# A new fixed order of all steps, and a new buffer table, for the two mixing stages of a two-layer hybrid decoder

## The chip, the core and the metric

The kernel runs on one core of one Trainium2 chip. Five engines work from queues of their own and in the order in which the program puts instructions into them: TensorE (PE, with its weight loads shown apart as PEld), VectorE (DVE), ScalarE (ACT), GpSimd (POOL) and SyncE (SP), which issues most transfers. An instruction waits at the head of its queue until the semaphores of what it needs are set; everything behind it in that queue waits too. The metric is the device time of one execution in microseconds, lower is better. Three runs of the kernel before took 1265.35, 1265.58 and 1265.79 us.

## The reference

Two layers over 512 tokens of width 1024, in float32. Each layer has a mixing stage and an MLP; the mixing stage runs three kinds of heads side by side on one input projection.

```python
for l in range(DEPTH):                                   # DEPTH = 2
    h = rms_norm(x, norm_mix_g[l])
    proj = h @ w_in[l]                                   # 1024 -> 3328 columns
    p_att, p_conv, p_rwkv = jnp.split(proj, ...)
    o_att = diff_attention(q, k, v, lam, ...)            # 6 heads of 64, two softmaxes each, causal
    o_conv = short_conv(b_gate, c_gate, u, conv_w[l])    # 256 channels, 3 taps
    o_rwkv = rwkv7_time_mix(p_rwkv, ...)                 # 6 heads of 64, a recurrence over 512 steps
    mixed = jnp.concatenate([o_att, o_conv, o_rwkv], axis=-1)
    x = x + mixed @ w_out[l]
    h = rms_norm(x, norm_mlp_g[l])
    x = x + jnp.square(jax.nn.relu(h @ w_mlp_up[l])) @ w_mlp_down[l]
return rms_norm(x, final_norm_g)
```

The recurrence of the third kind of head is, for each head and step,

```python
sa = einsum('bhvk,bhk->bhv', state, -kk_t)
state = state * w_t + sa (x) (kk_t * a_t) + v_t (x) k_t
y_t = einsum('bhvk,bhk->bhv', state, r_t)
```

## The kernel before

All activations lie transposed: 128 channels on the partitions, 512 tokens along the free axis, eight tiles `x0` to `x7` for the width of 1024. A product keeps float32's precision with three matmuls on rounded operands: weights and activations are split into a first part (`hi`, rounded by a cast on ACT) and a second part (`lo`, what is left, a subtraction on DVE or POOL), and PE adds hi*hi, hi*lo and lo*hi in PSUM. Weights come in groups of 128 output columns. Half a group (four blocks of 128 x 128, 256 KB) is loaded into a `raw` tile, cast to `whi` and subtracted to `wlo`; each of the three tiles has three buffers, so that at most three half groups are on their way.

A layer has two parts. The MLP is written out in plain loops. The mixing stage is written as generators, each of which yields after every instruction or small group of instructions (a *step*). The function `drive` takes a string, `ORDER[l]`, in which a letter stands for a generator and a number behind it for so many of its steps: `R2 m g3` is two steps of `R`, one of `m`, three of `g`. It calls the generators in that order, and so sets the order in every engine's queue. Between engines the string fixes nothing; the semaphores do. The letters:

- `d` the loads of raw weights and constants (SP), `w` the casts to `whi` (ACT), `x` and `y` the subtractions to `wlo` on DVE and on POOL (the string `LO` says which half group goes to which)
- `m` the products, one matmul a step: 888 in each stage, which are the input projection (`pj`, 624), the output projection in two halves of 96 (`po`), and the first three groups of the MLP (`up`, 72)
- `e`, `q`, `n` the scaling and the RMS norm of the input; `k` constants
- `g`, `h` the decay rates and the gate of the recurrence
- `A`, `B`, `C` three pairs of attention heads; `U`, `V` the two convolution tiles
- `R`, `S`, `T` three pairs of recurrent heads, and `r`, `s`, `t` the triangular inverse that each of them needs
- `o`, `i`, `p`, `N` the residual sums, the scaling and the norm of the MLP's input

An attention pair handles two heads of four blocks of 128 queries. For each block PE makes two score tiles (`sc`); DVE adds the causal mask and finds the maximum (line 1298), ACT takes the exponentials with their sums (L1305), DVE makes the factor of the second softmax (`sm`, L1307 and L1309, one column wide) and the difference `pp` (L1311); PE transposes it (`ptt`), ACT copies it out, and after four blocks PE multiplies with the values (`po` of the attention, with 64 columns).

A recurrent pair works in chunks of 64 tokens. Its matmuls are on 64 x 64 parts of PE's array: gram matrices (`pg`), then `pbv`, `pzw`, `pap`, `pbs`, `pyy`; between them stand transposes (`pk`, `pb`, `pa`, `pv`, `phy`) and the seven state updates (`pst`). The inverse uses 64 x 64 and 32 x 32 parts (`px`, `py`, `pz`, `pzz`) and, on POOL, thirty small operations. A pair ends with a gate product (`pgt`), the output `yc` (L1101 and L1108) and its two parts `mhi` and `mlo` (L851 and L852), which the output projection reads. The order of the output projection's blocks is `K_ORD`: its second half starts with the outputs of `S`, `V`, `C` and `T`, in this order.

Beside the order stands a table, `SLOTS[l]`: for each tag with several buffers the sequence of buffer numbers in which tiles take them, such as `wp/wlo 012012...` or `ps/rp` for the four PSUM banks that the small work shares. The products have PSUM banks of their own (`ps/mm`, two), and so has attention (`ps/at`, two).

Of the kernel before, what the change touches and what calls it, by code (L numbers as in the profile page):

```python
# [22 lines left out]
S = 512  # L23
# [3 lines left out]
C = 64  # L27
# [28 lines left out]
         "g d6 e d2 w e q m w m w x2 d m w m d x m q m d e m q d m q e d m e d m q2 m d e m e d m q d w m2 d e m w m d m x m d m w m x d m2 x d m q m "  # L56
         "d m e m q d m2 d e2 m2 q d m e m e m2 q m2 e2 m2 q m e m3 q m3 q m2 k5 m k q m3 k m k n k m n m n m2 n m n m n w m n m n x w d m n x m2 w m "
         "d m2 g y m5 k g m d g m k2 m2 k m k g m3 g m3 g m2 w m g m g m x m3 g3 d g m3 g3 m2 w g2 A m3 x A m3 d A m2 A m2 A m g m3 w g2 h y m2 g m R "
         "m3 g d g R2 m2 g m R m w m2 g2 m g2 x m g2 R d m g m A m R m R m h m A m R m w m2 A2 m R m y m A m R A2 m d R m R m R A m R2 m A m w m A m2 "
         "x A m3 d m2 R m2 R m R m w m2 R m y m5 R2 m d m3 w A R m A m x A6 m A2 m R d A m2 R A m A2 m2 A m2 R m w m2 R m2 y R A d A m A R m A R m A2 "  # L60
         "R m r A2 m A m A m R2 w r A m R r x A d R6 A R h R r3 A R2 m h R h m A m R A2 m A2 m R m A m r A m r m R2 m A m2 w m A m r m A R m r R A y "
         "m3 A m r A2 d R2 A r A m2 r m A r A m2 r B m w r m2 r R2 A y B A m2 R m r d m R A m r A R m r R r A B2 R2 r m B A2 h w r2 m r A m r m A x m2 "
         "A m r d m A r m2 r A3 m r A m A r A m2 r w m r S m A m r m x S m S m r A m d A m r m A r m S A m A2 m w A2 m A m A m x m A m2 d m A m r A m "
         "A m2 A h m2 w S m2 A2 x m S h A m S A d m2 r m2 r m2 r m w m r2 m3 A m2 y m2 A r A m d S m r m r A m h w m r S A y B m r S B r d A m2 r3 A m "
         "S A2 B2 m r S B A2 r B m r2 m r B m r A2 B m r S B S2 m r2 m w r m B R S x B S2 m d S R m2 A R S m3 S A m R A S A2 R2 m A2 R5 A m R m A R m "
         "w R m R m A R y m R A m R m A m R d A m A R m A m A R A m A m R A m w A R A m A m R y R d S m R S m R m2 R m2 R m S m R m2 S w S A x A d B S "
         "m S B A s S m S2 B R m s m3 A m s S m2 A m3 w S2 A R x S m S B m R m A R s3 m R m R S d S R A R m B R m S R m B A m S m B S2 R s B R m s S m "
         "B s w B2 s T s x m T2 m s B m d B m s B m T m B m2 s B m S m3 s w m B s m B S m s m y B m B2 m B2 m B m B s d m S2 m B m2 w m B T m2 s m S B "
         "S m s B m T s m T m x B m s B2 d m T B m2 s B w m s m B T m s m y m B T B s m d T m B s T m T m s m B m s B m s w m C m s B s m S C S m s T "
         "B C2 T B m B s B m C s m2 s B2 m s m x m B m2 R d m R w m2 B m y R s m R2 d B m S T S T B m S T s m B S s m T m s m w m s2 m B2 C S y R C S "  # L70
         "B R s C2 B d m s T m s C m T m C m s B C R S m C B s T m C S m s B3 m s2 m s m B m w C B m s C B y m s m s3 m B m s d B m B s B m s2 m B s m "
         "B2 S w B2 S m2 B2 m2 U m B m2 S m2 B m x m S B d B2 S m B S B S m w B2 m2 B m B m S m B m S m S2 m B S m B m S2 B m2 w m S B S2 x B2 m y S d "
         "B2 S m B m B m d m S B U2 m S m S m U B m S m S2 w B2 T m S B T S m S B2 S T S m T m T B S B2 m x B m T B d m T m2 B t T m2 T2 B m t m w m C "
         "m t m y m T m C T2 C d B m S T B m S B m S T B m t3 S B m T S T B S B S B m S T B m S B m w S B m S B m T S B m2 T2 t y B T m C B m2 t C m T "
         "m C m2 t w C m S m C T m2 t V C2 t C S C T d C m C S2 C m t C m S t m2 t m C t m C m t w m x C m C2 m t d C2 m t C m C t m2 x C m2 t m d C m "
         "C m t C w m t m U C U t m x m C2 m t C2 d m t m C2 m t m U m C m2 t w m U m2 C t m2 C t m C m U m2 C m C2 t x m C w m C t d m t m C t m C m "
         "t m x m C m t m V d m V t m C t m V m w m4 C m y C m4 t C d m C2 m C m t w m2 C m t m t m C m t2 m C m B m T m2 C3 B w T m2 C t T C x m C T2 "
         "C d t m C m t T2 U C x t T C d m T U C T m t C2 m t C2 T C2 m t C m3 t C m w C m C m t2 y V C T t m t2 m t C2 m T d C2 S t C m C S m C m3 t "
         "m C t2 m C m w o m2 V y m C m2 t T d V C T m T C2 m C2 m T C2 V C V C m T m T m w T m2 o V m y m T m2 T m T2 m d C m T m C m2 w T2 C o m C2 "
         "T2 x T V d m C m T m C m T C m T m C m T C3 m T m2 C T C w m C T2 o C x m C d T C m C T m C m C T m2 C m T m2 C T m C2 m2 w m T m C y m o C "  # L80
         "m3 C m T d m T m T C m3 T w m T o m3 T x m3 T d m T m T m T m T m w T m T m2 o y m T m T2 d m T m4 T m2 w m T m2 o y m6 d m3 w m o m2 y m p "
         "m3 i m2 d m i m2 w m o m3 x p m3 d i p m5 w m i m2 o m3 x m p m2 d m p m2 w m o m2 y m p m4 p m d m3 w m o m3 x p m3 d p m5 w m o m3 x p m3 "
         "d p m5 w m o m2 y m p m4 p m d m i m3 w o m3 i2 m2 p m i m i m p m3 w m i2 N x m i2 m d m i2 m2 i m3 N m x m2 w m3 y m5 N m N m N m N m w N "
         "m N y m N m34 ",
         "d3 w e x q d e w q y d w m4 x m3 d m e g m d m q m d e m w m2 q m2 y m n m d n m n m2 n m n m n m n w m n y m n m3 d g m3 g m g m3 w g m3 x "
         "m3 d m3 g m3 g m2 w g m2 g m x m3 g3 d g m3 g3 m w m g2 x m3 d m4 g m3 g h g w m g R g3 m R2 m4 g2 m g2 R m g2 h m g m h m2 x m h w m2 d m h "
         "x m3 h d m3 h m3 w m R m2 h y m6 R h d R m3 w m R m2 R x m3 R d m R m R m R m R5 m R m2 w A m R m R m3 A m x m3 R d m2 w m3 R m3 R m5 R m w "
         "m2 R m2 R A2 x A x m d R m d m R m R m r m R2 m r m w m2 R r m2 R2 m x R m2 R m d m R2 r3 m R m2 R A R2 w R m A m R m3 A2 m R m2 r A m x m A "
         "m R m w A m2 A m2 A r m x m d m2 r A m r m A2 m r A r w d m r m A2 r R m2 A r m x m R A R m2 A r m r m A R2 A m r m d R2 r w r A r A R m A r "
         "m A R m x m R2 A r d r A m r R A m R r m A m r A m r m A m r A2 m r A2 m r w A m r m S A m r m r A m x S m S m2 A r d m A r m A m r S m w A "  # L90
         "m2 A2 y m A2 m2 A2 m d m2 A m r m2 A m A w m A m3 x A m B d A2 m A2 B m2 A2 m2 r m A m2 r m w m r m2 A r2 m5 A m x r w A d m r m r B2 m A y "
         "S B r A2 r S d r S r m r2 A m2 S2 r A m r S A r3 A r S m A S2 A r A S2 m A r m A S m r m r A R A S2 A m A S R m2 w R S m2 S A m2 R y S d A R "
         "m A2 R m R A m R m2 R m w R2 m A m y R m R m R A2 m R m A R m d U R m2 R m A m A R A w m2 R A R y A2 m R A2 R m A2 d m2 R2 A3 S m R A S m R "
         "m2 R A R m A2 S m R A2 m w m2 R m y m3 A2 m2 d m R B A m3 R S w S B R A y m S m d R m A R m A m3 R B2 A m R A2 S B R S B s S B S B A R B s A "
         "m A m B R m A S m B w m R m B s m A m R m A R B m A B m x R A m d S2 R2 S s3 S A m A m S R S m A R m A m A m S A R m S m2 A S s S A w s m A "
         "s S m2 s m s m A m x m w m A d m s m A m2 y m A m B A m2 s d m S A m B m s m w B m A m S B m x m B m2 s d m S2 m B3 m B m B2 m s m B S m s m "
         "S m s B m B s m w B m s m S B S B2 x B m2 s C d m2 s w m B s m B m C s m S2 s B x B m s S m d B m C S m C m S s S C B s B s m S s B S m s B2 "
         "s m w B2 s m s m T m s m s B2 m T s m T x m2 B m T d m3 B w m B m B s m y m2 B m B2 d m B2 m2 B2 m2 s m B m2 s m w m s m2 s2 m2 T m3 y B m w "
         "s m s y d m s m2 s T B d m T B m2 s m s B T3 B s2 B s T8 s T B m2 s T m s3 m T m s C B m T s m s3 m C m S B C2 w m B C S y m C B3 S m2 C m B "
         "m C B2 S d B C w B C B2 C m S B m y S B2 S m B2 m2 B2 m S d m2 B S m S2 m B S m B m S2 w B m2 S m S y B S B2 m S B2 S d m B2 m2 S m B S m S "  # L100
         "m B m B S B m2 w m S B S y B T d B S B S T B m3 B m B m2 T m B m T m2 T B S w B S B m S T B x B2 T d T t T2 U B U2 m t B m B m T m t B m2 T "
# [1497 lines left out]
```

## Time and profile before

| what | us |
|---|---|
| median of three runs | 1265.58 |
| the profiled execution | 1265.92 |
| its span, first to last instruction | 1264.1 |
| first mixing stage, products from | 5.5 to 306.9 |
| second mixing stage, products from | 634.4 to 928.3 |
| VectorE busy | 912.8 |
| ScalarE busy | 697.3 |
| GpSimd busy | 334.6 |

The stages between and behind are the MLPs. In the rows of the profile, `pj<-ahim,whi` reads "writes `pj`, reads `ahim` and `whi`"; a matmul's duration includes its way through the array, so that consecutive matmuls overlap and the distance of their starts is what one costs. A row of a group ends with the idle time of the engine ahead of it and who ended it. The granted clock is a share of full speed.

### The profile page before, as it was taken

To read this page: it belongs to the slowest core of one execution; us is meant where nothing else is said; L and a number is where in the kernel's file an instruction comes from. 1 tells how busy PE (TensorE), PEld (TensorE's weight loads), DVE (VectorE), ACT (ScalarE), POOL (GpSimd) and SP (SyncE) were. 2 spreads that over 40 slices of the span, in tenths; PEclk is the share of its full clock that TensorE was granted. 3 is DMA by queue.
4 is the path that set the end of the run, shared out by engine and by line. 5 is a ranking of instruction groups with operands and counts; after the bars stand their busy time and mean duration, and the time that the engine had idled before them with its cause. 6 is when DMAs were issued, how large, how long until landed. Compare 5 with 4: busy or idle time off the path is not lost.

```text
span 1264.1 us, 25145 instructions
## 1 busy us (share of the span) xinstructions
PE 1242.0 (98%) x9493; PEld 1050.4 (83%) x9493; DVE 912.8 (72%) x1889; ACT 697.3 (55%) x1474; POOL 334.6 (26%) x433
## 2 busy tenths in 40 slices
PE   9999999999999999999999999999999999999997
PEld 6777777787789898989878787887787989898987
DVE  6788888867976666665667787879598766666654
ACT  6675655646744545444575656564575545454552
POOL 1343626133300101010224345352431010111110
PEclk9999999999999999999999999999999999999998
DMA  6533333142343333321235334332434333333122
GB/s 212 159 85 94 109 94 101 52 133 84 101 125 101 100 101 101 101 84 51 75 102 144 100 102 109 98 96 60 133 93 133 93 108 95 107 100 102 59 75 76
DMA packets 84410, 127.93 MB, mean 101 GB/s; under 512 B 21440, under 2 KB 25024, under 8 KB 84288
## 3 DMA queue, kind: packets, MB, share of 16 engines
q1 hardware_dynamic: 83568, 125.77, 32.7%
q8 instruction: 75, 1.23, 0.4%
q10 hardware_dynamic: 720, 0.55, 0.1%
q14 instruction: 47, 0.39, 0.1%
HBM read 117.11 MB, written 9.18 MB: 100 GB/s over the span
## 4 chain that ended last, share of the span: by engine, by line
PE 70%; DVE 4%; ACT 1%; issue 1%; DMA 0%; POOL 0%; DVEq 0%; ACTq 0%; POOLq 0%
PE dn L289 22%; PE pj L289 11%; PE pa L289 11%; PE pb L289 5%; PE up L289 5%; PE po L289 4%; PE dnF L289 3%; PE pc L289 3%; PE sc L289 1%; PE ptt L294 1%; PE pg L289 1%; DVE wlo L343 0%; DVE blo L1433 0%; DVE x L1509 0%; PE pyy L289 0%
## 5 line engine op out<-in xcount | busy, mean ns | idle before, releaser
L1377 POOL TENSOR_TENSOR ml<-m,mh 128x512 fp32r<-128x512 f32 x64 | 95.2, 1490 | 509.7 <-ACT mh L1376 491.7
L342 ACT CAST whi<-raw 128x512 fp32r<-128x512 f32 x142 | 88.2, 622 | 173.7 <-PE dn L289 155.8
L289 PE MATMUL dn<-mh,whi 128*128 128x512 f32 x448 | 175.3, 391 | 2.0 <-DVE x L1509 2.0
L289 PE MATMUL dn<-ml,whi 128*128 128x512 f32 x448 | 174.6, 390 | 0.0
L289 PE MATMUL dn<-mh,wlo 128*128 128x512 f32 x448 | 174.6, 390 | 0.0
L289 PE MATMUL pj<-ahim,whi 128*128 128x512 f32 x392 | 157.7, 402 | 4.4 <-DVE vf L1266 1.7
L289 PE MATMUL pj<-ahim,wlo 128*128 128x512 f32 x392 | 158.3, 404 | 0.0
L289 PE MATMUL pj<-alom,whi 128*128 128x512 f32 x392 | 158.1, 403 | 0.0
L662 ACT CAST whi<-raw 128x512 fp32r<-128x512 f32 x142 | 87.8, 619 | 93.4 <-PE pj L289 39.6
L671 POOL TENSOR_TENSOR wlo<-raw,whi 128x512 fp32r<-128x512 f32 x62 | 81.6, 1316 | 215.7 <-ACT whi L662 197.0
L1509 DVE TENSOR_TENSOR x<-dn,x 128x512 f32<-128x512 f32 x112 | 76.8, 686 | 76.8 <-PE dn L289 76.8
L343 DVE TENSOR_TENSOR wlo<-raw,whi 128x512 fp32r<-128x512 f32 x142 | 115.2, 812 | 11.2 <-ACT whi L342 11.2
L1448 DVE TENSOR_TENSOR slo_p<-s,shi_p 128x512 fp32r<-128x512 f32 x96 | 70.9, 741 | 63.4 <-ACT shi_p L1447 56.4
L289 PEld LDWEIGHTS dn<-mh,whi 128*128 128x128 f32 x448 | 84.1, 188 | 21.6 <-issue 2.5
L289 PEld LDWEIGHTS dn<-mh,wlo 128*128 128x128 f32 x448 | 84.1, 188 | 17.9
L289 PEld LDWEIGHTS dn<-ml,whi 128*128 128x128 f32 x448 | 84.1, 188 | 16.4
L289 PEld LDWEIGHTS pj<-ahim,whi 128*128 128x128 f32 x392 | 73.9, 188 | 19.8 <-issue 1.7
L1447 ACT CAST shi_p<-s 128x512 fp32r<-128x512 f32 x96 | 59.3, 619 | 50.4 <-PE pa L289 38.9
L289 PEld LDWEIGHTS pj<-ahim,wlo 128*128 128x128 f32 x392 | 73.8, 188 | 14.3 <-issue 0.9
L289 PEld LDWEIGHTS pj<-alom,whi 128*128 128x128 f32 x392 | 73.9, 188 | 14.1 <-issue 0.5
L289 PE MATMUL pa<-thi,shi_p 128*128 128x256 f32 x288 | 81.3, 282 | 0.5 <-DVE c L1493 0.5
L289 PE MATMUL pa<-tlo,shi_p 128*128 128x256 f32 x288 | 81.4, 282 | 0.0
(409 smaller groups left out, 3255.4 us busy)
## 6 DMA issues: line engine op xcount, KB each, us to landing
raw<-wts SPq DMA_DIRECT2D x391, 256.0 KB, 2.7
qs<-dqhi SPq DMA_DIRECT2D x24, 128.0 KB, 3.4
ks<-dkhi SPq DMA_DIRECT2D x24, 128.0 KB, 3.9
x<-xT SPq DMA_DIRECT2D x8, 256.0 KB, 4.6
dqhi<-qhi SPq DMA_DIRECT2D x6, 256.0 KB, 3.3
dqlo<-qlo SPq DMA_DIRECT2D x6, 256.0 KB, 3.2
dkhi<-khi SPq DMA_DIRECT2D x6, 256.0 KB, 2.7
dklo<-klo SPq DMA_DIRECT2D x6, 256.0 KB, 3.2
```

Of the source, the lines that this page charges most:

```text
L289: ins = nc.tensor.matmul(*a, **k)
L294: ins = nc.tensor.transpose(*a, **k)
L342: act.copy(hi[:, :n], raw[:, :n])
L343: (pool if a and lean[0] else dve).tensor_tensor(lo[:, :n], raw[:, :n], hi[:, :n].bitcast(F32), ALU.subtract)
L662: yield act.copy(hi[:, k0:k1], raw[:, k0:k1])
L671: yield eng.tensor_tensor(lo[:, :n], raw[:, :n], hi[:, :n].bitcast(F32), ALU.subtract)
L1377: pool.tensor_tensor(lo, m, hi.bitcast(F32), ALU.subtract)
L1447: act.copy(hi, src)
L1448: dve.tensor_tensor(lo, src, hi.bitcast(F32), ALU.subtract)
L1509: dve.tensor_tensor(x[j], pt, x[j], ALU.add)
```

## The change

It replaces the two strings `ORDER` and the two tables `SLOTS`. Nothing else in the program differs: the generators, the split of `wlo` between DVE and POOL, the loads and their sizes stay. The numbers of steps per letter are the same in both strings. The first lines of each, and the place in the second stage that the prediction names:

```diff
 ORDER = (
-         "g d6 e d2 w e q m w m w x2 d m w m d x m q m d e m q d m q e d m e d m q2 m d e m e d m q d w m2 d e m w m d m x m d m w m x d m2 x d m q m "
-         "d m e m q d m2 d e2 m2 q d m e m e m2 q m2 e2 m2 q m e m3 q m3 q m2 k5 m k q m3 k m k n k m n m n m2 n m n m n w m n m n x w d m n x m2 w m "
...
-         "d3 w e x q d e w q y d w m4 x m3 d m e g m d m q m d e m w m2 q m2 y m n m d n m n m2 n m n m n w m n y m n m3 d g m3 g m g m3 w g m3 x "
...
+         "g d6 e d2 w e q m w e2 w m w x m2 d x2 m5 e d w2 d q2 e d2 q d q2 d2 m7 q2 m5 e2 w d2 m3 x d2 q3 d q2 m e2 m3 e k2 m7 k2 m2 q m4 x q m3 e x "
+         "m n2 d2 m3 n m n4 m3 k2 d2 k e4 n w x w x m11 n d2 m3 k m3 g5 m8 g7 m2 d R m2 g2 k m6 w m4 R m3 R2 w R x y m2 A g4 m4 g R2 d g3 m g A m2 w "
...
+         "d3 w e x q d e w q y d w m10 q2 m x m7 d e2 g n2 w m5 y m n m n2 d n2 m n2 g m2 g d2 g m5 w g2 m2 y m12 w m d m4 x w m h2 m5 g3 m g3 d x R "
...
+         "m7 R4 A3 m R g2 m3 R d R x w d2 A m R2 m2 r3 m r m2 x m6 R r2 d A R3 A R w A R m2 w m2 r3 R m5 R A x r3 A5 R4 A3 r2 A m11 R x R A4 m w m3 "
...
 SLOTS = (
...
-         "cp/rr 01 "
-         "cp/rst 01201201 "
+         "cp/rr 10 "
+         "cp/rst 01201210 "
...
-         "mp/tp 01234510245234513512041025023524520013000341351302 "
+         "mp/tp 01234510224524212153041351351505032142424251201240 "
...
-         "ps/rp 01233303103102310231023102310231023102021301230123012032121023102310202130123012301230123012013201313021032 "
+         "ps/rp 01233301230123013201302130130123012301013203203210323201321302130213030123102310231023102313130213030123102 "
...
-         "wp/wlo 01201201201201201201201201201201201201201201201201201201201201201201 "
+         "wp/wlo 01201021012021012012012012012102012012012021021021021201201201201201 "
```

Every other line of both strings is replaced as well, and the buffer sequences of the tags `mp/ks`, `mp/qs`, `mp/mix`, `mp/pe1`, `ps/at`, `ps/mm`, `wp/raw`, `wp/sq` and `wp/whi` in one or both stages.

More of the change, by code (lines that the diff above doesn't have):

```diff
@@ L115 @@
          "cp/ro 010 "
-         "cp/rr 01 "
-         "cp/rst 01201201 "
-         "cp/rsx 01201201 "
+         "cp/rr 10 "
+         "cp/rst 01201210 "
+         "cp/rsx 01201210 "
          "cp/ry 010 "
@@ L128 @@
          "mp/dc 010 "
-         "mp/ks 101010 "
+         "mp/ks 010101 "
          "mp/lw 012 "
-         "mp/mix 01201210 "
+         "mp/mix 01210021 "
          "mp/mx 012301230123012301230123012301230123012301230123 "
          "mp/oss 010 "
-         "mp/pe1 01010010100 "
+         "mp/pe1 01010010101 "
          "mp/pp 011001100110011001100110011001100110011001100110 "
-         "mp/qs 101010 "
+         "mp/qs 010101 "
          "mp/s0q 010 "
@@ L140 @@
          "mp/tc 010110 "
-         "mp/tp 01234510245234513512041025023524520013000341351302 "
+         "mp/tp 01234510224524212153041351351505032142424251201240 "
          "mp/tq 010101010101 "
          "mp/ty 010101010 "
-         "ps/at 010101010101010101010101010101010101010101010101010101010101010101010101010101010101 "
-         "ps/mm 01011101010001010101010101010101010101010 "
-         "ps/rp 01233303103102310231023102310231023102021301230123012032121023102310202130123012301230123012013201313021032 "
+         "ps/at 101010101010101010101010101010101010101010101010101010101010010101010101010101010101 "
+         "ps/mm 01011101010001010101011010101010101010101 "
+         "ps/rp 01233301230123013201302130130123012301013203203210323201321302130213030123102310231023102313130213030123102 "
          "wp/raw 01201201201201201201201201201201201201201201201201201201201201201201201201 "
-         "wp/sq 010100001010101 "
+         "wp/sq 101010001010101 "
          "wp/whi 01201201201201201201201201201201201201201201201201201201201201201201 "
-         "wp/wlo 01201201201201201201201201201201201201201201201201201201201201201201 ",
+         "wp/wlo 01201021012021012012012012012102012012012021021021021201201201201201 ",
          "cp/rk 010 "
@@ L153 @@
          "cp/rr 01 "
-         "cp/rst 01201201 "
-         "cp/rsx 01201201 "
+         "cp/rst 01201210 "
+         "cp/rsx 01201210 "
          "cp/ry 010 "
@@ L170 @@
          "mp/oss 010 "
-         "mp/pe1 01010101010 "
+         "mp/pe1 01001010101 "
          "mp/pp 011001100110011001100110011001100110011001100110 "
@@ L177 @@
          "mp/tc 010100 "
-         "mp/tp 01234510245235423143150241324125123504132413453420 "
+         "mp/tp 01234510245452545151230452145234213052431243023014 "
          "mp/tq 010101010101 "
@@ L181 @@
          "ps/at 010101010101010101010101010101010101010101010101010101010101010101010101010101010101 "
-         "ps/mm 01010100101010101010110101010101010101010101 "
-         "ps/rp 01230123012301230123012301231023102021301230123012301230123021032121302310231023013201320123012323102130 "
-         "wp/raw 01201201201201201201201201201201201201201201201201201201201201201201201201 "
-         "wp/sq 010101010 "
-         "wp/whi 01201201201201201201201201201201201201201201201201201201201201201201201201 "
-         "wp/wlo 01201201201201201201201201201201201201201201201201201201201201201201201201 ")
+         "ps/mm 10101011010101010101001010101010101010101010 "
+         "ps/rp 10321032103210210213021302130231023230120312031023012301230120312020132130213021302130213021302121032013 "
+         "wp/raw 12012012012010210210210210210210210210210210210210210121021021201201201021 "
+         "wp/sq 101010101 "
+         "wp/whi 21021021021021021021021021021021021021021021021021021021021021021021021021 "
+         "wp/wlo 21021021021020120120120120210210210210210210210210210121021021201201201021 ")
 NG = NG_IN + NG_OUT + NG_UP + NG_DN
```

90 rows, old and new, of the table ORDER are left out of this document.

## The prediction

> **What bounds the kernel now.** I read the page's busy table and its chain of work first, then the busy time by stage, the waits of TensorE, and a few timelines.
>
> ```profile
> span 1264.1 us, 25145 instructions
> PE 1242.0 (98%) x9493; PEld 1050.4 (83%) x9493; DVE 912.8 (72%) x1889; ACT 697.3 (55%) x1474; POOL 334.6 (26%) x433
> PE 70%; DVE 4%; ACT 1%; issue 1%; DMA 0%; POOL 0%; DVEq 0%; ACTq 0%; POOLq 0%
> ```
>
> PE is busy 98% of the span and makes up most of the chain that ends last. No order can shorten its arithmetic; it can only close gaps and make the instructions follow one another more tightly.
>
> ```profile
> core 0: us, PE busy (x) PEld busy (x) DVE busy (x) ACT busy (x) POOL busy (x), PEclk, DMA share, GB/s
> 0.00:22.00 22.00, 19.51 (x73) 12.65 (x74) 14.86 (x31) 14.92 (x26) 1.16 (x5) 1.00 0.84 268
> 22.00:306.00 284.00, 278.66 (x2731) 222.41 (x2732) 220.64 (x553) 171.66 (x403) 116.64 (x179) 1.00 0.34 101
> 640.00:928.00 288.00, 285.99 (x2774) 230.73 (x2775) 217.98 (x554) 171.20 (x403) 113.85 (x178) 1.00 0.36 105
> ```
>
> These are start-up and the two mixing stages, the only places that the change orders. PE is idle 284.00 - 278.66 = 5.3 us in the first and 288.00 - 285.99 = 2.0 us in the second; the granted clock is 1.00, so the throttle plays no part. VectorE (DVE) is busy 76 to 78% there, so a step that arrives late on it meets a queue. Which waits those idle microseconds are:
>
> ```profile
> engine line waited for: us in total, times, longest us
> PE ptt L294 <- DVE pp L1311: 2.7, 4, 0.9
> ...
> PE pj L289 <- DVE vf L1266: 1.7, 2, 0.9
> ...
> PE pj L289 <- DVE pg L784: 1.1, 1, 1.1
> ...
> PE pj L289 <- DVE pk L784: 0.7, 1, 0.7
> ...
> PE pj L289 <- DVE kf L1239: 0.4, 1, 0.4
> ```
>
> Nine waits, 2.7 + 1.7 + 1.1 + 0.7 + 0.4 = 6.6 us, all for DVE. Four are the transposes of an attention block (`ptt`) waiting for the block's last DVE step; five are products (`pj`) whose PSUM buffer DVE had not emptied. None is a wait for a cast weight. How the longest came about:
>
> ```profile
> start us, us, engine line op out<-in xcount [idle before <-releaser]
> 84.89 1.27 POOL L1156 TENSOR_TENSOR ee<-nn,cst 128x512 f32<-128x512 f32 x1
> 84.92 1.26 DVE L1309 SCALAR_TENSOR_TENSOR sm<-s0q,nlam,sm 128x1 f32<-128x1 f32 x1
> 86.21 0.35 DVE L1311 SCALAR_TENSOR_TENSOR pp<-sc,sm,pp 128x128 f32<-128x128 f32 x1
> 86.62 0.33 PE L294 MATMUL ptt<-cst,pp 128*128 128x128 f32 x1 [0.86 <-DVE pp L1311]
> ...
> 854.62 1.32 DVE L1309 SCALAR_TENSOR_TENSOR sm<-s0q,nlam,sm 128x1 f32<-128x1 f32 x1
> 854.65 1.28 POOL L671 TENSOR_TENSOR wlo<-raw,whi 128x512 fp32r<-128x512 f32 x1 [2.49 <-ACT whi L662]
> ```
>
> ```profile
> L1309 DVE SCALAR_TENSOR_TENSOR sm<-s0q,nlam,sm x48: 179/220/1319, 59.0 to 871.8; 128x1 f32<-128x1 f32 x48
> ```
>
> The DVE step on a single column takes 0.22 us (median) but 1.26 and 1.32 us where a POOL operation on a whole tile runs beside it, and it ends with that operation. About 1.06 us is added, and the transposes behind it wait. So a good part of today's waiting is a collision of two engines at a place that depends on both queues.
>
> **The change part by part.** Both order strings spend every generator's steps exactly once: 2,249 steps in the first stage and 2,196 in the second, with the same 1,945 PE instructions in each. Nothing is added or removed; the sum has three terms.
>
> *First: how often PE changes between products and small work.* Counted along the strings, the runs of small work between products fall from 134 to 79 and from 124 to 80. What that is worth:
>
> ```profile
> 103.15 0.20 PE L289 MATMUL pzz<-xs,rt 32*32 32x32 f32 x2
> 103.28 0.51 PE L289 MATMUL pj<-ahim,whi 128*128 128x512 f32 x1
> 103.62 0.40 PE L289 MATMUL pj<-alom,whi 128*128 128x512 f32 x1
> 103.85 0.40 PE L289 MATMUL pj<-ahim,wlo 128*128 128x512 f32 x1
> ...
> 108.83 0.30 PE L289 MATMUL pbs<-vt,kt 64*64 64x64 f32 x6
> 109.05 0.66 PE L294 MATMUL ptt<-cst,pp 128*128 128x128 f32 x4
> ...
> 844.26 0.39 PE L289 MATMUL pj<-alom,whi 128*128 128x512 f32 x1
> 844.58 0.90 PE L289 MATMUL pbv<-vt,kq 64*64 64x64 f32 x31
> 845.27 0.27 PE L289 MATMUL px<-yi,ee 64*64 64x64 f32 x3
> ...
> 846.74 0.60 PE L294 MATMUL ptt<-cst,pp 128*128 128x128 f32 x4
> ```
>
> Products start every 0.23 us (103.62 to 103.85). After a group on part of the array (64*64 or 32*32) the second product starts 0.34 us after the first (103.28 to 103.62): leaving such a group costs 0.11 us. Entering it costs 0.32 - 0.23 = 0.09 us (844.26 to 844.58). Transposes right behind such a group take 0.66 instead of 0.60 us for four, a loss of 0.06; one such group behind another (`px` behind `pbv`) pays nothing. Full-array transposes and matmuls save next to nothing by moving together: what the following product loses, the missing tail makes up. In the strings, partial-array groups followed by products fall from 25 + 27 = 52 to 7 + 8 = 15: 37 x 0.11 = 4.1 us saved. In their place 21 more are followed by transposes or the like (21 x 0.06 = 1.3 lost), 8 more by scores or other full-tile matmuls (8 x 0.11 = 0.9 lost), and 8 more stand behind one another (8 x 0.09 = 0.7 saved). Sum: -4.1 + 1.3 + 0.9 - 0.7 = -2.6 us. Bounds: 0, if PE merely waits longer for the same data, and -4.8, if the 2.2 us of losses do not arise.
>
> The Trainium skill (TensorEngine Tiling (Array Packing), Key Properties) says that a change of the tiling mode drains the array, whatever follows. By that alone only the 8 groups behind one another save anything, 8 x (0.11 + 0.09) = 1.6 us in place of 2.6; the 0.66 against 0.60 us of the transposes agrees in direction, but the loss is half as large there as in front of products.
>
> *Second: the nine waits.* The distance in PE work between an attention block's scores and its transposes grows, summed over 24 blocks, from 87 to 101 us in the first stage and from 82 to 96 in the second (counted along the strings, a product at its 0.23 us, small work at its spacing in the timeline). That is the link of the four `ptt` waits. I take all nine as gone, -6.6 us; the bounds are -6.6 and 0.
>
> *Third: what is late next.* The casts lose their lead. For each half group I walked back from the first product that needs the second part of its weights (`wlo`) to the latest small PE work that anything ahead of that cast in its engine's queue depends on, and summed the PE work between. The median falls from 9.3 to 7.4 us and from 9.4 to 7.0; casts with under 4 us rise from 0 to 10 of 68 and from 2 to 12 of 74. The thinnest stands in the second stage, at `g2 m3 R d R x w d2`: from the end of the gram matmuls PE has 5 products and 2 matmuls, 7 x 0.23 = 1.6 us, until the second part of group 3 is needed, while DVE has two steps on `pg` and the cast behind them:
>
> ```profile
> L952 DVE TENSOR_TENSOR nn<-pg,rk 128x256 f32<-128x256 f32 x12 | 4.7, 416 | 0.9 <-PE pg L289 0.9
> ...
> L671 DVE TENSOR_TENSOR wlo<-raw,whi 128x512 fp32r<-128x512 f32 x80 | 56.3, 705 | 6.0 <-ACT whi L662 5.4 <-PE pb L294 0.2
> ```
>
> ```profile
> L671 POOL TENSOR_TENSOR wlo<-raw,whi 128x512 fp32r<-128x512 f32 x62 | 81.6, 1316 | 215.7 <-ACT whi L662 197.0 <-PE pj L289 7.7 <-DVE mlo L852 2.7
> ```
>
> ```profile
> L662 ACT CAST whi<-raw 128x512 fp32r<-128x512 f32 x142 | 87.8, 619 | 93.4 <-PE pj L289 39.6 <-PE po L289 24.7 <-issue 17.7
> ```
>
> 2 x 0.42 + 0.71 = 1.5 us against 1.6: just in time, with nothing over. Behind a late cast the whole product stream waits, and every chain with it. Price of one such wait: the nearest rows are the `ptt` waits, 2.7 / 4 = 0.68 us. Bounds: none of the 22 thin casts is late (0), or all (22 x 0.68 = 15.0 us). I take six, 4.1 us: two thirds of the nine waits of now, since most thin casts keep half a microsecond or more over their steps.
>
> *Edits that I cost at nothing.* The loads move later: their lead, by the same walk, falls behind the first three groups from 13.2 to 8.0 us and from 15.3 to 9.2.
>
> ```profile
> raw<-wts SPq DMA_DIRECT2D x391, 256.0 KB, 2.7
> ```
>
> A load and its casts need 2.7 + 0.62 + 1.32 = 4.6 us, so products hide them; were that cover gone, each would cost its 0.68. On SyncE's queue the bounces of queries, keys and the inverse stand behind other loads than before: those held up longest wait for 8.5 us of PE work instead of 7.2, which their chains' slack takes up. The buffer table only names which of the same buffers each tile takes. The head and the tail keep their work and nearly their order; start-up (19.51 of 22.00 us busy, DMA share 0.84) hangs on the loads of `x`.
>
> **Sum.** -2.6 - 6.6 + 4.1 = -5.1 us. Against the profiled execution (1264.1 us of span, 1265.9 in all, which is 0.3 above the median of 1265.6) that is 1260.8; against the median 1260.5, which I predict.
>
> **Rivals.**
> *No wait comes back:* 1265.6 - 2.6 - 6.6 = 1256.4. For it: the chains' distances grew. Against: the thin casts.
> *The gain is waited for at the end:* the second half of the output projection needs the last attention and recurrence outputs. In the old string their last steps stand at 693 and 721 of the 888 products, in the new at 727 and 730, and products 726 to 731 are the first that need them. If that is what ends the stage, the -5.1 vanish in one wait: 1265.6. Against it:
>
> ```profile
> L1108 DVE SCALAR_TENSOR_TENSOR yc<-yc,prm,pgt 128x512 f32<-128x512 f32 x6 | 4.4, 738 | 0.7 <-PE pgt L289 0.6
> ...
> L852 DVE TENSOR_TENSOR mlo<-yc,mhi 128x512 fp32r<-128x512 f32 x6 | 4.1, 689 | 0.8 <-ACT mhi L851 0.7
> ```
>
> ```profile
> L851 ACT CAST mhi<-yc 128x512 fp32r<-128x512 f32 x6 | 3.7, 618 | 3.2 <-DVE yc L1108 3.0
> ```
>
> Behind the last gate matmuls (at product 717) come 0.74 + 0.62 + 0.69 = 2.05 us of steps, and PE has 13 products, 3.0 us, until it needs the last of them.
>
> *Slower, by casts just in time:* POOL and DVE collide at other places than before, and a hold of 1.06 us eats the lead of a thin cast. All 22 late: 1265.6 - 9.2 + 15.0 = 1271.4. It decides from 17 of them on (17 x 0.68 = 11.6, over the 9.2 saved and 2.5 more). For it: DVE at 76 to 78% and 1.5 us of steps in 1.6 us. Against: most of the thin casts had the room counted above.
> By the Trainium skill (SBUF — State Buffer, SBUF: two separate sides), VectorE operations with two SBUF inputs and GpSimd operations exclude one another for a whole instruction; the two rows at 84.89 and 84.92 agree. By that rule a search that times steps one by one from an old trace carries the holds to wrong places, which is the supply of this rival.
>
> **How the numbers follow.** Forecast (1257.5 to 1263) 0.40; no wait back (below 1257.5) 0.13; waited for at the end (1263.1 to 1268.1) 0.17; slower 0.30. About 0.2%, 2.5 us, is what a measurement of this kernel tells from no change. So faster 0.53, within 0.17, slower 0.30. The range of 8 in 10 runs from 1254.5, the no-wait case with the larger gain from switching (1265.6 - 4.8 - 6.6 = 1254.2, rounded inwards), to the slower rival's 1271.4; the forecast's own range stands beside it.
>
> **What would show it.** Right: PE idle under 5 us in the two mixing stages together, `ptt` waits mostly gone, about 160 runs of small work, PE's busy time 2 to 3 us less, and the waits that remain naming `wlo` or `whi`. Wrong: waits for casts over 9 us in sum; the last products of a stage waiting for `mlo`; or a first stage whose start-up is longer.

## The result and the profile after

The changed kernel takes 1294.62 us (median of four runs, 1292.74 to 1299.24) against 1265.68 of the kernel before in the same measurement: a ratio of 1.0234, with a 95% interval of 1.0207 to 1.0262. It is slower by 29 us, outside the range of the prediction. The profiled execution took 1295.29 us.

The page of the changed kernel, its span, busy times and chain of work:

```profile
span 1293.5 us, 25133 instructions
PE 1247.0 (96%) x9493; PEld 1056.7 (82%) x9493; DVE 949.1 (73%) x1889; ACT 701.5 (54%) x1482; POOL 339.9 (26%) x433
PE 73%; DVE 16%; issue 3%; ACT 3%; DMA 1%; POOL 1%; SPq 0%; DVEq 0%; ACTq 0%; POOLq 0%
```

The span grew by 29.4 us. PE's idle time (span less busy) went from 22.1 to 46.5 us, 24.4 of them; its busy time grew by 5.0 with the same 9493 instructions. VectorE is busy 36.3 us longer, also with the same 1889 instructions, and its part of the chain went from 4 to 16%. An engine that does the same work in more time is the first thing to explain.

Busy time by stage, in the columns of the prediction's view (the second stage starts 14 us later than before, so its window is moved by that):

```profile
0.00:22.00 22.00, 14.71 (x46) 9.18 (x47) 8.24 (x14) 10.80 (x19) 1.81 (x8) 0.84 0.66 211
22.00:306.00 284.00, 271.61 (x2684) 218.28 (x2684) 228.22 (x551) 170.60 (x400) 110.13 (x171) 0.99 0.35 100
654.00:942.00 288.00, 271.70 (x2692) 218.77 (x2691) 228.67 (x531) 160.18 (x388) 113.98 (x176) 0.99 0.34 101
```

PE's idle time was 2.5, 5.3 and 2.0 us in these three; now it is 7.3, 12.4 and 16.3. Start-up manages 46 matmuls in 22 us where it had 73. The waits of PE:

```profile
engine line waited for: us in total, times, longest us
PE ptt L278 <- DVE pp L1295: 7.3, 10, 1.9
PE pj L273 <- DVE wlo_s L655: 4.8, 1, 4.8
PE pot L278 <- DVE ot L1320: 3.2, 4, 2.1
PE pj L273 <- DVE wlo L655: 3.2, 2, 2.4
PE px L273 <- DVE yi L1142: 2.6, 2, 1.7
PE pj L273 <- DVE pv L768: 2.5, 1, 2.5
PE pg L273 <- DVE ysum L1073: 2.3, 1, 2.3
...
PE pj L273 <- ACT ahim L422: 1.8, 1, 1.8
```

The product waits for `vf`, `pg`, `pk` and `kf` are gone, as forecast, but one of 2.5 us for `pv`, made by the same line as `pg` and `pk`, has come. The waits for `pp` grew from 2.7 to 7.3 us. The new ones lie all over the small work, nearly all for a DVE step, and one of 4.8 us (`wlo_s`) stands in the head. Waits for the cast weights behind the head are 3.2 us for DVE's (`wlo`) and 0.5 us for POOL's.

**Where in the time.** The starts of the same product in both traces give the delay: 4.1 us at the 3rd, 10.5 at the 49th, 16.2 at the end of the first mixing stage, 13.9 at the first product of the second (the MLP between gives 2.3 back), 29.5 at its end. So the head costs some 10 us, the rest of the first stage 6, the second stage 16.

**The head.** The timeline of the changed kernel, start-up:

```profile
8.66 0.72 ACT L422 ACTIVATE ahim<-x,prm 128x512 fp32r<-128x512 f32 x1 [2.84 <-DMA x<-xT]
9.29 1.12 ACT L646 CAST whi_s<-raw 128x512 fp32r<-128x512 f32 x2
9.42 0.75 DVE L423 SCALAR_TENSOR_TENSOR alom<-x,prm,ahim 128x512 fp32r<-128x512 f32 x1 [3.93 <-ACT ahim L422]
10.09 1.28 DVE L655 TENSOR_TENSOR wlo_s<-raw,whi_s 128x512 fp32r<-128x512 f32 x2
10.83 0.80 PE L273 MATMUL pj<-ahim,wlo_s 128*128 128x512 f32 x1 [4.78 <-DVE wlo_s L655]
```

In the kernel before, the first second part of the weights is made at 5.79 us:

```profile
5.79 0.69 DVE L671 TENSOR_TENSOR wlo_s<-raw,whi_s 128x512 fp32r<-128x512 f32 x1 [0.37 <-ACT whi_s L662]
```

The new string has `w e2 w m w x` where the old one had `w m w x2`. `e2` is the scaling of the second tile of `x`, on ACT (`ahim`) and DVE (`alom`); that tile lands at 8.66 us. The subtraction `x`, whose data had long been there, stands behind it in DVE's queue, and two casts of weights stand behind it in ACT's.

**The held steps.** The timeline of the changed kernel at two of the waits; `x2` marks two instructions in one row:

```profile
57.53 1.72 POOL L655 TENSOR_TENSOR wlo<-raw,whi 128x512 fp32r<-128x512 f32 x1
58.04 3.44 DVE L655 TENSOR_TENSOR wlo<-raw,whi 128x512 fp32r<-128x512 f32 x2
59.21 1.73 POOL L902 TENSOR_TENSOR bb<-kkn,av 128x512 f32<-128x512 f32 x1
59.85 0.50 PE L273 MATMUL pj<-ahim,wlo 128*128 128x512 f32 x1 [2.39 <-DVE wlo L655]
...
752.78 1.44 DVE L906 SCALAR_TENSOR_TENSOR ar<-kkn,dx 128x512 f32<-128x512 f32 x1
754.83 1.28 POOL L907 TENSOR_TENSOR bk<-bb,di 128x512 f32<-128x512 f32 x1 [1.16 <-issue]
755.19 1.47 DVE L908 TENSOR_TENSOR ar<-zr,dx 128x512 f32<-128x512 f32 x1
756.06 3.40 POOL L655 TENSOR_TENSOR wlo<-raw,whi 128x512 fp32r<-128x512 f32 x2
756.58 1.76 DVE L909 TENSOR_TENSOR bk<-k,di 128x512 f32<-128x512 f32 x1
758.26 1.74 DVE L1229 TENSOR_TENSOR klo<-kf,khi 128x512 fp32r<-128x512 f32 x1
760.52 1.44 PE L273 MATMUL pg<-ar,bk 64*64 64x128 f32 x32 [2.29 <-DVE ysum L1073]
```

A DVE step on a whole tile takes about 0.7 us; beside POOL's operations these take 1.44 to 1.76. POOL's take 1.72 where they took 1.28: both engines alternate, each waiting for the other's whole instruction. Four whole-tile steps between 752.8 and 758.3 lose 0.7 to 1.1 us each, and PE stands idle for 2.29 us ahead of the gram matmuls behind them. In the groups of DVE the same work shows as

```profile
L655 DVE TENSOR_TENSOR wlo<-raw,whi 128x512 fp32r<-128x512 f32 x80 | 64.1, 808 | 15.3 <-ACT whi L646 15.0
```

against 56.3 us and a mean of 705 ns before, for the same 80 subtractions.

**A wait that is not a hold.** ScalarE loads a table (`ACT_TABLE_LOAD`, 1.28 us) where its steps change from one function to another. The old order has 11 such loads and the new one 19, 10.3 us more, though ScalarE's busy time grew by 4.2 us in all. Ahead of the longest `ptt` wait, `av`, a step of the recurrence, stands between the two exponentials of one attention block, and costs two loads there:

```profile
70.41 1.28 ACT L814 ACT_TABLE_LOAD   x1
71.71 0.69 ACT L814 ACTIVATE av<-pa,prm 128x512 f32<-128x512 f32 x1
72.42 1.28 ACT L1289 ACT_TABLE_LOAD   x1
73.71 0.37 ACT L1289 ACTIVATE sc<-pp,mx 128x128 f32<-128x128 f32 x1
75.10 0.33 PE L278 MATMUL ptt<-cst,pp 128*128 128x128 f32 x1 [1.94 <-DVE pp L1295]
```

### The profile page after: what moved, and what is told of

It is laid out like the page before. It is cut to its first block, busy times and chain, and to the rows that moved or that the text cites. A ratio compares the mean times of both kernels' runs of the same rounds, so it can differ in the third digit from the quotient of the medians.

```text
span 1293.5 us, 25133 instructions
## 1 busy us (share of the span) xinstructions
PE 1247.0 (96%) x9493; PEld 1056.7 (82%) x9493; DVE 949.1 (73%) x1889; ACT 701.5 (54%) x1482; POOL 339.9 (26%) x433
## 4 chain that ended last, share of the span: by engine, by line
PE 73%; DVE 16%; issue 3%; ACT 3%; DMA 1%; POOL 1%; SPq 0%; DVEq 0%; ACTq 0%; POOLq 0%
PE dn L273 22%; PE pj L273 12%; PE pa L273 11%; PE po L273 7%; PE pb L273 5%; PE dnF L273 3%; PE pc L273 3%; PE up L273 2%; DVE wlo L327 1%; DVE wlo L655 1%; PE ptt L278 1%; PE sc L273 1%; DMA raw<-wts 1%; DVE sm L1293 1%; DVE pp L1282 1%
## 5 line engine op out<-in xcount | busy, mean ns | idle before, releaser
L655 POOL TENSOR_TENSOR wlo<-raw,whi 128x512 fp32r<-128x512 f32 x62 | 84.9, 1372 | 227.3 <-ACT whi L646 206.8
```

Of the source, the lines that this page charges most:

```text
L655: yield eng.tensor_tensor(lo[:, :n], raw[:, :n], hi[:, :n].bitcast(F32), ALU.subtract)
```

## The experiments

Two theories stand: **(H) the head**, an order of queues at start-up, worth about 10 us; **(P) the holds**, DVE steps that wait for POOL's operations (and POOL's that wait for DVE's), worth most of the rest. The rival to P is that the new order is worse by its own distances or its buffer table, whatever the lengths of the steps. Ratios are always to the kernel before on the same chip. Line numbers shift with the length of the strings.

**The first stage alone.**

```diff
-ORDER = (old first stage, old second stage)     SLOTS likewise
+ORDER = (new first stage, old second stage)
```

> New order and table in the first mixing stage, the old ones in the second. By the times of the products in the two traces the changed kernel is 16.2 us behind at the end of the first stage, gets 2.3 back in the MLP behind it, and loses 15.6 in the second. If the two stages' losses are independent, this kernel is 13 to 15 us slower than before (about 1279.5). If the first stage only hands on a state that makes the second one slow, it is as slow as the changed kernel (1293).

Measured: 1279.53 us, ratio 1.0109 (1.0094 to 1.0124), 13.9 us over the kernel before: what the delays in the trace said. With the 15.6 us that the second stage loses in the trace (29.5 less 13.9) this makes the whole loss, so the two stages' losses add up.

**The old head.** The old order up to the 72nd product of the first stage, the new one for all that is left; the buffer table follows the order.

> The changed kernel with the old order up to the 72nd product of the first stage (slots worked out anew), the new one behind it. Theory head: VectorE's second scaling stood ahead of the first second part and waited for a transfer, which blocked VectorE, and through the buffers the loads; 9 to 10 us come back (about 1284). Rival: the chip's start is what it is and the later waits take the gain back, under 3 us.

Measured: 1284.01 us, ratio 1.0148 (1.0133 to 1.0163). The head is worth 1.0234 - 1.0148 = 0.0086, 10.9 us. H stands as to size. VectorE's busy time stays at 949.1 us, so the other 18.7 us are a matter by themselves.

**No reads on POOL, new and old order.** In the mixing stages, POOL's whole-tile operations read only two columns (of each block of weights), followed by fills of the whole tile. The values of those tiles (second parts of the weights and of `pd`, `k`, `bb`, half of `bk`, inputs of the inverse, the convolution's products, the norm's sum) are left out; order, table and number of tiles stay.

```diff
+def filled(out, a, b, op, value=0.0):
+    cut = lambda t: t[(slice(None),) * (len(t.shape) - 1) + (slice(0, 2),)]
+    pool.tensor_tensor(cut(out), cut(a), cut(b), op)
+    for _ in range(3):
+        ins = pool.memset(out.bitcast(F32), value)
+    return ins
```

> The changed kernel in which GpSimd's operations on whole tiles in both mixing stages (second parts, recurrence inputs, convolution, norm sum) read two columns and fill the rest with a constant, three fills of about the same total length; their values are left out, the waits kept. Theory holds: VectorE's operations are no longer held by GpSimd's reads, VectorE's busy time falls from 949 by 35 us or more, and the time falls by 12 to 16 us to about 1280, the head's 10 us staying. Rival, thin casts and short distances: under 4 us.

> The kernel before with the same fills in place of GpSimd's whole-tile operations. Theory holds: the old order has few collisions (VectorE's steps held by over 0.3 us: 23 against 59), so that it gains 2 to 5 us, mostly the three transposes that waited behind a held step. Rival: it gains as much as the new order, 12 us or more, because the fills shorten something else.

Measured: 1287.14 us, ratio 1.0161 (1.0144 to 1.0178) for the new order; 1275.18, 1.0077 (1.0061 to 1.0092) for the old, which was to become faster and became 9.5 us slower. VectorE's busy time fell to 901.1 and 898.5 us, so most of the held time is gone in both. But the substitute is too long: a small operation and three fills take 0.22 + 1.69 = 1.9 us where one operation took 1.28. POOL's busy time in the old order rises from 334.6 to 393.3 us, and PE waits for POOL's own chains (`pssf`, 3.7 us in two waits). The pair cannot be read as a price; only its difference of 0.0084 can, and it mixes two effects.

**The same with two fills**, so that POOL's steps keep their length (its busy time is 327.6 and 328.4 us), in the new and the old order, and in the new order behind the old head.

```diff
-    for _ in range(3):
+    for _ in range(2):
```

> As the run of the changed kernel with fills, but two fills and the two-column operation (about 1.35 us) in place of three (1.9 us), against 1.28 us of the operation that they stand for. The values of GpSimd's whole-tile operations are left out. Theory holds: with the length right, the order that lost 29 us keeps the head's 10.6 and little else: 1276 to 1281. Rival, distances too short by themselves: above 1285.

> The kernel before with the same two fills. Theory holds: 1261 to 1265, two to five under before; the 9.5 us that three fills cost came from 0.6 us more on each GpSimd step. Rival: the fills cost by their other effects, and it stays above 1270.

> Old order up to the 72nd product, the new one behind it, two fills for GpSimd's whole-tile operations (values left out). If head and holds are the whole loss, it is within 3 us of the kernel before with the same fills, or below it by the 2.6 us of fewer switches that were forecast (1260 to 1266). If the new order loses by itself, it stays 8 us or more above that.

| order | POOL reads (as it is) | POOL reads two columns | the holds are worth |
|---|---|---|---|
| old | 1 (1265.6 us) | 0.9969 [0.9958, 0.998] | 0.0031, 3.9 us |
| new behind the old head | 1.0148 [1.0133, 1.0163] | 0.9936 [0.992, 0.9951] | 0.0212, 26.8 us |
| new | 1.0234 [1.0207, 1.0262] | 1.0014 [1.0003, 1.0025] | 0.0220, 27.8 us |

P stands: the holds cost the new order 27 us and the old one 4. The head costs 10.9 us with them and 9.9 without, the same within the intervals, so the two hardly touch. Without both, the new order is ahead of the old one by 0.0033, 4.2 us, the intervals just apart: taken together, its distances and its buffer table are not worse. So the ratio of 1.0234, 29.6 us, is made up of 9.9 us for the head and 27.8 - 3.9 = 23.9 us for the holds, less 4.2 us for all else.

Single places of the new order are worse even so. With POOL reading two columns PE waits 3.4 us for `pp` behind the old head (2.0 of them at the place of the two table loads) and 5.4 us in the new order; in the old order it is 0.5 us. The wait for `pv` stays too, at 1.9 and 1.8 us. The pages of the old order and of the new one behind the old head, both with two fills:

```profile
PE 1241.0 (98%) x9493; PEld 1050.8 (83%) x9493; DVE 897.6 (71%) x1889; ACT 696.7 (55%) x1474; POOL 328.4 (26%) x673
```

```profile
PE 1234.5 (98%) x9493; PEld 1056.8 (84%) x9493; DVE 899.1 (71%) x1889; ACT 701.3 (56%) x1482; POOL 329.5 (26%) x673
```

VectorE now takes the same time in both orders. So 912.8 - 897.6 = 15 us of its busy time were holds in the kernel before, and about 949.1 - 899.1 = 50 in the changed one. PE is busy 6.5 us less in the new order, which fewer switches to parts of the array would bring about; but with the holds the same order and head have 1241.9 us, so PE's busy time also moves by 7.4 us without any change of switches, and the 6.5 us are not shown to be theirs.

**A step that isn't held.** The kernel before, with the factor of the second softmax written with one tensor and two scalar columns.

```diff
-dve.scalar_tensor_tensor(sm[:, 2:3], s0, nlam[:, l:l + 1], sm[:, 2:3], ALU.mult, ALU.mult)
+dve.tensor_scalar(sm[:, 2:3], sm[:, 2:3], s0, nlam[:, l:l + 1], ALU.mult, ALU.mult)
```

> The kernel before with the factor of the second softmax (one column wide, 48 times) made by an operation with one tensor input and two per-partition scalars in place of one with two tensor inputs. Theory: only operations that read two tensors are held, so the column step is never longer than 0.3 us, the three transpose waits behind it (2.5 us) go, and the time falls by 1 to 3 us. Rival: this form is held as well, and nothing changes.

Measured: 1264.00 us, ratio 0.9985 (0.9976 to 0.9994), the fastest kernel here that computes everything. The steps and what PE still waits for them:

```profile
L1309 DVE TENSOR_SCALAR sm<-sm,s0q,nlam x48: 231/273/276, 59.0 to 869.9; 128x1 f32<-128x1 f32 x48
```

```profile
PE ptt L294 <- DVE pp L1310: 1.4, 2, 0.9
```

The longest of 48 is 276 ns where it was 1319, and the transposes' waits halve from 2.7 to 1.4 us.

> The kernel of e2 (old order up to the 72nd product of the first stage, new order behind it) with the factor of the second softmax written with one tensor and two scalar columns. If the holds of this step matter in the new order as in the old one, where they were worth 1.6 us, its transposes' waits (6.2 us in e2) fall by half or more and the time is 3 to 5 us under e2's 1284.0: 1279 to 1281. If the wide steps' holds set the time, within 1 us of e2: 1283 to 1285.

The same edit in the new order behind the old head: 1283.81 us, ratio 1.0139 (1.0122 to 1.0155). This is the second outcome: by the ratios 1.1 us less than the kernel without it, which is not to be told from nothing, though VectorE is busy 7.5 us less (941.6) and the `ptt` waits fall from 6.2 to 4.1. The holds of the wide steps, which stay here and are gone in the table above, carry most of the price.

**Where in the head.** Two kernels move one letter of the new head; a third takes the old order for the first 24 products and the new one behind them.

```diff
-"g d6 e d2 w e q m w e2 w m w x m2 d x2 m5 e d w2 d q2 ..."      changed kernel
+"g d6 e d2 w e q m w2 m w x m e2 m d x2 m5 e d w2 d q2 ..."      scaling behind one second part
+"g d6 e d2 w e q m w2 m w x m2 d x2 e2 m5 e d w2 d q2 ..."      behind all three
```

> The changed kernel with one letter moved: the second tile's scaling (e2) stands behind the first product that needs a second part, `w w m w x m e2 m d x2` in place of `w e2 w m w x m2 d x2`; the buffer table follows. If the head's 10.6 us come from this one place (the first second part and the casts queued behind a scaling whose tile of x lands at 8.6 us), the third product starts near 6 us and 7 to 10 us come back: 1284.5 to 1287.5. If the loss is spread over the whole head (norm, constants, loads), less than 4 us: over 1290.5.

> As e9, but the second tile's scaling stands behind all three first second parts: `w w m w x m2 d x2 e2 m5` in place of `w e2 w m w x m2 d x2 m5`. In e9 the second and third subtraction still stood behind it, so that the third reload of raw weights, and the last four tiles of x behind it in SyncE's queue, went out at 11.65 us instead of 9.45. If that chain (VectorE's queue, the raw buffers, SyncE's queue, x) carries the head's loss, the tiles of x go out near 9.5 us and 5 us or more of the 10.6 come back: 1284 to 1290. If the later places of the head (norm, scalings and casts behind the 9th product) waste what is won again, as in e9, less than 3 us: over 1291.5.

> The old order up to the 24th product of the first stage (e2 had it up to the 72nd), the new order behind it. If the loss lies in the start itself (first second parts, reloads, tiles of x), nearly all that e2 won comes back: 1284 to 1287. If it lies in the norm and scalings behind, where ScalarE's casts stand behind squares and scalings, less than half: over 1289.

Measured: 1296.50 us, ratio 1.0235 (1.022 to 1.025); 1293.18, 1.0223 (1.0206 to 1.024); 1289.91, 1.019 (1.0175 to 1.0205). Set against 1.0234, 0, 1.4 and 5.6 us come back of 10.9; the first two are not to be told from nothing. The delay of the nth product to the kernel before, in us, from the starts of the `pj` rows:

| product | changed | behind one | behind three | old first 24 | old first 72 |
|---|---|---|---|---|---|
| 3rd | 4.1 | -0.3 | -0.3 | -0.2 | -0.3 |
| 10th | 4.0 | 1.7 | -0.4 | -0.1 | -0.3 |
| 21st | 4.8 | 3.3 | 2.6 | -0.1 | -0.3 |
| 37th | 7.5 | 5.9 | 5.0 | 1.7 | -0.3 |
| 49th | 10.5 | 8.6 | 7.7 | 5.7 | -0.3 |

The two moves did what they should at their place: the 3rd product is back in time, and with the second move the tiles of `x` go out at 9.57 us instead of 12.38. But the time won is waited away at the next place. My expectation that one place carries the head was wrong. What stands next, with the old first 24 products:

```profile
14.41 0.63 ACT L380 ACTIVATE sqm<-x 128x512 f32<-128x512 f32 x1 [0.74 <-DVE wlo_s L600]
15.08 0.69 DVE L383 TENSOR_TENSOR accm<-accm,sqm 128x512 f32<-128x512 f32 x1
15.80 0.64 ACT L380 ACTIVATE sqm<-x 128x512 f32<-128x512 f32 x1 [0.76 <-DVE accm L383]
16.47 0.69 DVE L383 TENSOR_TENSOR accm<-accm,sqm 128x512 f32<-128x512 f32 x1 [0.70 <-ACT sqm L380]
17.20 0.63 ACT L380 ACTIVATE sqm<-x 128x512 f32<-128x512 f32 x1 [0.76 <-DVE accm L383]
17.73 1.32 ACT L367 ACTIVATE ahim<-x,prm 128x512 fp32r<-128x512 f32 x2
...
18.49 0.49 PE L218 MATMUL pj<-ahim,whi_s 128*128 128x512 f32 x1 [1.63 <-ACT ahim L367]
```

A square on ACT waits for DVE's addition of the one before, and DVE for the square, 1.4 us a turn; the scaling that PE waits for stands behind three such turns. The old string puts two scalings behind each square, so that ACT works while DVE adds:

```profile
13.98 0.63 ACT L451 ACTIVATE sqm<-x 128x512 f32<-128x512 f32 x1
14.52 1.32 ACT L438 ACTIVATE ahim<-x,prm 128x512 fp32r<-128x512 f32 x2
15.75 0.62 ACT L451 ACTIVATE sqm<-x 128x512 f32<-128x512 f32 x1
```

How the last 5 us split between these turns and the norm's other steps was not tried.

## Why the prediction was wrong

**The head at no cost: this step failed.** "The head and the tail keep their work and nearly their order; start-up ... hangs on the loads of `x`" was a reading of totals. The work is the same, but the changed string puts instructions that wait for loads of `x` in front of others that don't: behind one `e2` stood a subtraction, two casts, the raw buffers, SyncE's queue and four more tiles of `x`. The head cost 9.9 to 10.9 us where 0 was put down. No single place carries it: moving that `e2` gave back 0 to 1.4 us, the old order of the first 24 products 5.6, and the rest came with the old order up to the 72nd. The walk that gave the casts' leads was made from small PE work back, and there is none in the head.

**The second term, -6.6 us: this step failed.** Nine waits were taken as gone because their distances in PE work grew. The five product waits are gone (`vf`, `pg`, `pk`, `kf`), with 2.5 us for `pv` in their place; the `ptt` waits went from 2.7 to 7.3 us. A distance in PE work helps only while the steps that must fit into it keep their length, and they did not: held time on VectorE went from 15 to about 50 us. That is not all of it. "Nothing is added or removed" holds for the steps, but not for ScalarE's table loads, which went from 11 to 19; and with the holds taken away `ptt` waits of 3.4 to 5.4 us are left where the old order has 0.5. The distance summed over 24 blocks did not show the single blocks that became tight.

**The third term, +4.1 us for casts: near in size, by luck.** Waits for second parts of weights behind the head came to 3.2 us on VectorE, in two waits of 2.4 and 0.8 instead of six of 0.68, and to 0.5 us on POOL. Holds made a good part of them: with POOL reading two columns, 1.1 us of the longer one is left (1.6 behind the old head), and the other is gone. The larger new waits are those of chains with several DVE steps (`pot`, `px`, `pv`, `pg`, `phy`), as at 752.8 to 760.5 us above.

**The first term, -2.6 us: right in direction, its size not shown.** The price of a switch holds in the changed trace: behind a group on part of the array the second product still starts 0.34 us after the first. With holds and head taken away the new order is 4.2 us ahead of the old one, against a sum of -5.1 that also held the other two terms. PE's busy time is 6.5 us less there, more than the bound of 4.8, but it moves with the holds as well, and no run separates the switches from the rest.

**The slower rival had the right supply, with a place and a price too small.** The sum had no term for new holds; holds cost 23.9 us more than in the old order, the largest part of the loss. The rival let them eat the leads of 22 casts at 0.68 us, 15.0 at most, and counted 1.06 us for one hold. (Its "from 17 of them on" is 18 by its own figures: 11.6 is still under 9.2 + 2.5 = 11.7.) The prediction quoted the rule of the Trainium skill (SBUF — State Buffer, SBUF: two separate sides) that a VectorE operation with two SBUF inputs and a GpSimd operation exclude one another for a whole instruction. The runs agree: with POOL reading two columns, VectorE's same 1889 instructions take 899 instead of 949 us. The supply of such overlaps was thus VectorE's steps with two inputs in SBUF at large, and not one column and some casts: about 50 us of held time in the changed kernel, 35 more than before. That the new order meets more of them than the old could not be seen in the profile of before; why it meets three times as much is still open. Durations taken from a trace of another order hold that order's holds, and this fits, but was not tried.

*The gain waited for at the end* did not occur: PE never waited for `mlo`. Of the signs named ahead, "a first stage whose start-up is longer" showed; PE idle under 5 us, `ptt` waits mostly gone and a lower PE time did not.

## What to carry to other kernels

When an order is replaced, read its first 30 steps queue by queue: for each instruction that waits for a transfer, list what stands behind it on its engine and could have run. A distance between a producer and a consumer is worth only as much as the durations in it are stable; where VectorE and GpSimd share whole-tile work, price every two-input step of a chain with and without the hold. Count ScalarE's table loads in the new order as well: they are work that no step of the program names. And a substitute that removes a suspected cost must keep the duration of what it replaces: the three-fill version showed a gain and a loss at once, the two-fill version gave the price.

## What was not expected of the hardware

**A stall costs clock as well.** The changed kernel's windows around its longest wait and behind it:

```profile
10.80:13.00 2.20, 2.17 (x5) 1.80 (x6) 1.18 (x2) 0.24 (x1) 0.00 (x0) 0.50 0.52 142
13.00:16.00 3.00, 3.00 (x11) 2.36 (x11) 0.00 (x0) 1.54 (x3) 0.00 (x0) 0.74 0.94 320
```

Behind the 4.78 us of waiting the granted clock is 0.50, and products start every 0.43 us (11.42 to 11.85) instead of 0.23 until about 14.4 us. Over the whole execution the mean clock is 0.991 against 0.997: 1293.5 x 0.009 - 1264.1 x 0.003 = 7.8 us, an upper bound on what this added, since part of it falls where PE would have waited anyhow. Besides the head there are three more stretches at 0.50, of 3.4 us each (24.8 to 28.2, 76.0 to 79.4, 762.1 to 765.5), close behind waits of 1.81, 1.94 and 2.29 us; the kernel before has 1.00 in these windows. In the 3.4 us ahead of each of the three, PE was busy for 1.5 to 1.6 us. Where the limit lies was not tried. The Trainium skill (TensorE: Matmul & The Clock Gate, Part 1: The HAM clock gate) says that an idle array falls back to half its clock and needs some 3.4 us of activity to leave it; the rows agree in both, with about 3.6 us here (10.83 to 14.4). That PE's busy time rose by 5.0 us although it switches less fits this.

**Not only steps with two inputs are held,** against what was expected before the one-column step was rewritten. A copy of 64 x 4 in the changed kernel:

```profile
745.92 1.29 POOL L655 TENSOR_TENSOR wlo<-raw,whi 128x512 fp32r<-128x512 f32 x1 [8.36 <-ACT whi L646]
746.15 1.26 DVE L883 COPY rk<-rk 64x4 f32<-64x4 f32 x2
```

The first of the two takes 1.08 us, where one takes 0.15 at best, and ends with POOL's operation; the one-column step with one tensor and two scalars never was held in 96 cases.
